# Neighbourhood-head low parts at the later place before step 32, and the addition of a head's output put off behind the maxima

## The chip, the cores and the metric

The program runs on one core of one Trainium2 chip. A core has a matrix engine (PE; its weight loads are shown apart as PEld), a vector engine (DVE), a scalar engine (ACT), a general engine (POOL) and a queue that issues transfers (SP). Each works through its own list of instructions in the order in which they were written, and waits for another engine only where a semaphore says so. The metric is the device time of one execution in microseconds (us).

## What is computed

One encoder block on 1024 tokens of width 1024, in float32. A layer norm is followed by one projection, whose columns are queries, keys and values of two attentions and two gates. The attentions run side by side: neighbourhood attention on a 16 x 64 grid (8 heads), and attention in a window of 128 tokens with 8 query heads on 2 key heads. Their outputs are projected, gated and added; a projection, a layer norm, a squared-ReLU MLP and a last layer norm follow. The change concerns the attentions alone:

```python
qa, ka, va, qb, kb, vb, ga, gb = jnp.split(proj, IN_SPLITS, axis=-1)
y_na = neighbourhood_attention(qa, ka, va, na_rpb[l]) @ w_branch_na[l]
y_swa = windowed_gqa_with_sink(qb, kb, vb, swa_sink[l]) @ w_branch_swa[l]
mixed = jax.nn.sigmoid(ga) * y_na + jax.nn.sigmoid(gb) * y_swa
# each attention, for one head:  p = softmax(q k^T / 8 + bias or mask);  o = p v
```

## The kernel before

**High and low parts.** To keep float32 accuracy, an operand of a matrix product is split in a rounded high part and the remainder, the low part: a product of the projection is three products (high by high, high by low, low by high).

**Heads and steps.** The 16 heads (8 of the window, then 8 of the neighbourhood) are worked through in 64 steps, four to a head; each handles two blocks of 128 queries. They overlap as a pipeline, written out by hand. `steps(s, n)` writes, in this order: `part_a2(s+1)` (reciprocal of the sums, L593, and scaling of the probabilities, L596), `part_a(s+2)` (scores on PE, L559 and L560; on DVE the bias is added and the maximum taken, L562, and the maxima become the exponent's offsets, L568 or L566), some matmuls of the projection, an early place where deferred work may run, `part_b(s)` (PE turns the probabilities round, L618; ACT copies them as a high part, L621; DVE subtracts for the low part `ptl`, L624) with the exponentials of step s+2 on ACT (L580, L583) between copy and subtraction, a first later place for deferred work, more matmuls, `part_c(s-1)` (probabilities times values, L654), a second later place, and the rest of the matmuls. Below, a step that "handles" k is the one whose scores are those of step k.

**What fills PE between.** `pump` writes projection matmuls (L283) of the heads to come: 12 in each step up to s = 29, 18 in each after that. `defer(n, f)` puts `f` off until n such matmuls are written; `flush` then runs it at the next place. An entry marked early may also run at the early place, ahead of `part_b`; others run only at the two later ones.

**The head's output.** Every second step two blocks of `part_c` are complete in one `ps_o` bank: the product with the high parts of the values in rows 64 to 127, with the low parts in rows 0 to 63. ACT copies one half (`evac`, L660) and DVE adds the other (`evac2`, L663), both into `oT`. There are two `ps_o` banks, used by turns; the same holds for the banks of scores (`ps_s`), of turned probabilities (`ps_t`) and of the projection (`ps_mm`).

**The neighbourhood heads' queries and keys.** When half a block of `proj_na_qk` is complete in a `ps_mm` bank, `evac` copies its high parts (ACT, L353 to L355), and `evac2`, four matmuls later, makes the low parts (DVE: L358, L360, L362).

Of the kernel before, what the change touches and what calls it, by code (L numbers as in the profile page):

```python
# [47 lines left out]
D_NA = 4  # L48
# [35 lines left out]
def encoder_block(ctx, tc, x, w_in, w_br, w_out, w_ff1, w_ff2, par, rows, rpbp,  # L84
# [4 lines left out]
    def b32(ap):  # L89
        return ap.bitcast(F32)  # L90
# [12 lines left out]
    def psum(tag):  # L103
        return pp.tile([P, 512], F32, tag=tag, name=f"ps_{tag}", bufs=PSB[tag])
# [153 lines left out]
    def h_perm(part, k, half):  # L258
        return hT[:, part, k, half * 512:(half + 1) * 512]
# [17 lines left out]
    def gemm3_steps(ps, w, act):  # L277

        hi, lo = w[:2]
        for k in range(NK):  # L280
            for i, (a, b) in enumerate(((hi, 0), (hi, 1), (lo, 0))):
                yield
                PE.matmul(ps, a[:, k, :], act(b, k), start=(k == 0 and i == 0), stop=(k == NK - 1 and i == 2))  # L283
# [6 lines left out]
    def defer(*fns, pe=False, early=False):  # L290

        later.append([fns[0], fns[1:], pe, early])

    def flush(pe=True, early=False):
        for e in list(later):
            if e[0] <= 0 and (pe or not e[2]) and (e[3] or not early):
                later.remove(e)
                e[1][0]()
                if e[1][1:]:
                    defer(*e[1][1:], early=e[3])  # L300
# [40 lines left out]
    def proj_na_qk(h, w, store):  # L341
        q = ap.tile([P, S], F32R, tag="q", name="q", bufs=3)
        kh = ap.tile([P, S], F32R, tag="kh", name="kh")
        kl = ap.tile([P, S], F32R, tag="kl", name="kl")
        store.append((q, kh, kl))
        bq, bk = prm[0:64, C_QK + h:C_QK + h + 1], prm[64:P, C_QK + h:C_QK + h + 1]
        for half in range(2):
            cs = slice(half * 512, (half + 1) * 512)
            ps = psum("mm")
            yield from gemm3_steps(ps, w, lambda part, k: h_perm(part, k, half))  # L350

            def evac(cs=cs, ps=ps):
                ACT.activation(q[0:64, cs], ps[0:64, :], AF.Identity, bias=bq, scale=1.0)  # L353
                ACT.activation(kh[64:P, cs], ps[64:P, :], AF.Identity, bias=bk, scale=1.0)
                ACT.activation(kh[0:64, cs], ps[64:P, :], AF.Identity, bias=bk, scale=1.0)  # L355

            def evac2(cs=cs, ps=ps):
                DVE.scalar_tensor_tensor(out=q[64:P, cs], in0=ps[0:64, :], scalar=bq, in1=b32(q[0:64, cs]),  # L358
                                         op0=ALU.add, op1=ALU.subtract)
                DVE.scalar_tensor_tensor(out=kl[64:P, cs], in0=ps[64:P, :], scalar=bk, in1=b32(kh[64:P, cs]),  # L360
                                         op0=ALU.add, op1=ALU.subtract)
                DVE.tensor_copy(kl[0:64, cs], b32(kl[64:P, cs]))  # L362
            defer(0, evac, D_NA, evac2, early=True)


    mk = ap.tile([P, 640], F32, tag="mk", name="mk", bufs=1)
# [20 lines left out]

    n_rope = [0]
    in_steps, rope_ops = [], []

    def rope_step(p):

        if rope_ops:
            j = cp.tile([P, 1], F32, tag="junk", name="junk", bufs=2)
            POOL.tensor_copy(j, p[:, 0:1])
            rope_ops.pop(0)()
            if len(rope_ops) % 5 == 1:
                rope_ops.pop(0)()
                if rope_ops:
                    defer(8, rope_ops.pop(0))  # L400
# [147 lines left out]
    def part_a(s):  # L548

        hd, t = heads[s // 4], s % 4  # L550
        (q, kh, kl), _, _, bias_of, sink_h, _, _ = hd.get()
        st = ap.tile([P, 8], F32, tag="st", name="st", bufs=4)
        pns = []
        for i in range(2):
            j = 2 * t + i
            c0, c1 = max(j - 1, 0), min(j + 2, 8)
            n = (c1 - c0) * P
            ps = psum("s")
            PE.matmul(ps[:, :n], q[:, j * P:(j + 1) * P], kh[:, c0 * P:c1 * P], start=True, stop=False)  # L559
            PE.matmul(ps[:, :n], q[:, j * P:(j + 1) * P], kl[:, c0 * P:c1 * P], start=False, stop=True)  # L560
            p = ap.tile([P, 384], F32, tag="ss", name="ss", bufs=6)
            DVE.tensor_tensor_reduce(out=p[:, :n], in0=ps[:, :n], in1=bias_of(j), scale=1.0, scalar=NEG,  # L562
                                     op0=ALU.add, op1=ALU.max, accum_out=st[:, i:i + 1])
            pns.append((p, n, c0))
        if sink_h is None:
            DVE.tensor_scalar(out=st[:, 2:4], in0=st[:, 0:2], scalar1=-0.125, scalar2=None, op0=ALU.mult)  # L566
        else:
            DVE.tensor_scalar(out=st[:, 2:4], in0=st[:, 0:2], scalar1=snk8[:, sink_h:sink_h + 1],  # L568
                              scalar2=-0.125, op0=ALU.max, op1=ALU.mult)
        hd.pairs[t] = pns, st  # L570
# [14 lines left out]
    def part_a2(s):  # L585
        if s >= 64:
            return
        hd, t = heads[s // 4], s % 4
        pns, st = hd.pairs[t]
        sink_h = hd.get()[4]  # L590
        if sink_h is not None:
            DVE.tensor_tensor(out=st[:, 4:6], in0=st[:, 4:6], in1=st[:, 6:8], op=ALU.add)
        DVE.reciprocal(out=st[:, 6:8], in_=st[:, 4:6])  # L593
        for i in range(2):
            p, n, c0 = pns[i]
            DVE.tensor_scalar(out=p[:, :n], in0=p[:, :n], scalar1=st[:, 6 + i:7 + i], scalar2=None, op0=ALU.mult)  # L596
        rope_step(p)
# [29 lines left out]
    def part_c(s):  # L627

        hd, t = heads[s // 4], s % 4
        order, pth, ptl = hd.pairs[t]  # L630
        _, vv, vi, _, _, o_chunk, o_row = hd.get()
        if t % 2 == 0:
            hd.po = psum("o")
        po = hd.po

        runs = []
        for u, (c, i) in enumerate(order):
            if runs and runs[-1][0] == c:
                runs[-1][2] += 1
            else:  # L640
                runs.append([c, u, 1, i])
        runs.sort(key=lambda r: -r[2])
        runs.append(runs.pop(1))
        cols_ = (t % 2) * 256
        nmm = 0
        for c, u, w, i in runs:
            cc = slice(cols_ + i * P, cols_ + (i + w) * P)
            vs = vv[:, c, vi, :, :].rearrange("p a f -> p (a f)")
            main = (po[:, cc], vs, pth[:, u:u + w, :].rearrange("p u f -> p (u f)"))
            corr = (po[0:64, cc], vs[:, 0:64], ptl[:, u:u + w, :].rearrange("p u f -> p (u f)"))  # L650
            nmm += 1
            lastrun = nmm == len(runs)
            for m in ((corr, main) if lastrun else (main, corr)):
                PE.matmul(*m, start=(nmm == 1 and m is main), stop=(lastrun and m is main))  # L654
        if t % 2 == 1:

            oo = oT[o_row:o_row + 64, o_chunk, (t // 2) * 512:(t // 2 + 1) * 512]

            def evac():
                ACT.copy(oo, po[64:P, :])  # L660

            def evac2():
                DVE.tensor_tensor(out=oo, in0=po[0:64, :], in1=oo, op=ALU.add)  # L663
            if s == 63:
                last_evac.extend((evac, evac2))
            else:
                evac()
                defer(0, evac2)

    def fills():  # L670
        def na_v_of(hp):
# [28 lines left out]
    with tc.manual_schedule(engines=MANUAL):  # L700
# [22 lines left out]
        def pump(n):  # L723
            for _ in range(n):
                if next(fill, "end") == "end":
                    for e in later:
                        e[0] = 0
                    flush()
                    return
                for e in later:  # L730
                    e[0] -= 1
# [52 lines left out]
        def steps(s, n, before_b=None, before_c=None):  # L784

            part = [int(n * SPLIT[0]), int(n * SPLIT[1])]
            part.append(n - sum(part))
            if 0 <= s + 1 < 64:
                part_a2(s + 1)
            if s + 2 < 64:  # L790
                part_a(s + 2)
            pump(part[0])
            if before_b:
                before_b()
            flush(False, True)
            if 0 <= s < 64:
                part_b(s, lambda: part_e(s + 2))
            elif s < 0:
                part_e(s + 2)
            flush(False)  # L800
            pump(part[1])
            if before_c:
                before_c()
            if s >= 1:
                part_c(s - 1)
            flush()
            pump(part[2])
# [1253 lines left out]
```

## Time and profile before

| what | value |
|---|---|
| median of 3 runs | 1334.39 us (1333.94 to 1335.63) |
| the profiled execution | 1334.06 us, of which the span of the profile 1332.3 us |
| busy share of the span | PE 98%, PEld 82%, DVE 74%, ACT 53%, POOL 21% |
| granted PE clock | 0.998 over the span |

The heads take about the stretch from 91 to 460 us: the 12-matmul steps until some 250 us, the 18-matmul steps after. In a row of the timeline stand the start, the duration, the engine, the line, the operation, the tile written and those read, and in brackets how long the engine sat idle before it and which engine's work ended that. Matmuls are pipelined, so a matmul's duration overlaps the next one's, and what PE takes is read from the distance of starts.

### The profile page before, as it was taken

What the parts mean: (1) busy time and instruction counts of PE and PEld (TensorE: products, weight loads), DVE (VectorE), ACT (ScalarE), POOL (GpSimd) and SP (SyncE); (2) the same over time, 40 slices, a digit from 0 to 9 for tenths busy, and PEclk for the clock granted to TensorE, in tenths of its full rate; (3) what the DMA queues carried; (4) which work ended last, traced back from release to release, by engine and by line L of the source; (5) the groups of instructions that cost most, each with busy time, mean ns of one, the idle gap of its engine ahead of it and who ended that gap; (6) DMA issues with size and microseconds to landing.
All of it is one profiled execution on the core that took longest, in us unless ns stands there. A gap on an engine that the chain in (4) does not pass through costs nothing.

```text
span 1332.3 us, 17348 instructions
## 1 busy us (share of the span) xinstructions
PE 1309.4 (98%) x6296; PEld 1088.7 (82%) x6296; DVE 985.0 (74%) x1618; ACT 710.1 (53%) x1231; POOL 282.4 (21%) x279
## 2 busy tenths in 40 slices
PE   8999998999999999999999999999999999999997
PEld 6788787888888878888888888888888888888886
DVE  7758888877877896444678987677655768787778
ACT  6446666766665535542445755555555543333346
POOL 4441221121120000344540012222100001111207
PEclk9999999999999999999999999999999999999999
DMA  6521111102101323656143576655528644544323
GB/s 226 187 87 49 48 52 41 38 23 47 51 23 40 127 94 118 223 190 221 70 152 134 169 242 205 210 196 187 205 100 311 221 190 150 213 150 174 127 103 127
DMA packets 66422, 183.94 MB, mean 138 GB/s; under 512 B 10400, under 2 KB 12064, under 8 KB 60576
## 3 DMA queue, kind: packets, MB, share of 16 engines
q1 hardware_dynamic: 65904, 182.38, 39.7%
q8 instruction: 49, 0.80, 0.3%
q10 hardware_dynamic: 432, 0.46, 0.1%
q14 instruction: 37, 0.30, 0.1%
HBM read 126.69 MB, written 56.31 MB: 137 GB/s over the span
## 4 chain that ended last, share of the span: by engine, by line
PE 80%; DVE 12%; ACT 3%; issue 1%; POOL 1%; DMA 1%; SPq 0%; DVEq 0%; ACTq 0%; POOLq 0%
PE ps_mm L283 13%; PE ps_mm L1351 7%; PE ps_t L1351 6%; PE ps_o L1351 6%; PE ps_mm L1784 6%; PE ps_s L1784 6%; PE ps_o L1784 5%; PE ps_t L1784 5%; PE ps_s L1351 3%; PE ps_t L618 2%; DVE ss L562 2%; PE ps_o L654 2%; ACT ss L580 2%; PE ps_mm L886 1%; DVE ss L596 1%
## 5 line engine op out<-in xcount | busy, mean ns | idle before, releaser
L283 PE MATMUL ps_mm<-hT,whi 128*128 128x512 f32 x832 | 269.5, 398 | 2.6 <-POOL hT L255 2.1
L283 PEld LDWEIGHTS ps_mm<-hT,whi 128*128 128x128 f32 x832 | 153.6, 188 | 30.2 <-POOL hT L255 3.5
L283 PE MATMUL ps_mm<-hT,wlo 128*128 128x512 f32 x416 | 166.9, 401 | 1.0 <-DVE wlo L717 1.0
L580 ACT ACTIVATE ss<-ss,st 128x384 f32<-128x384 f32 (+1 forms) x128 | 74.5, 583 | 62.1 <-DVE st L568 47.3
L1650 ACT CAST t<-stg 128x2048 fp32r<-128x2048 f32 x28 | 53.5, 1912 | 81.9 <-PE ps_o L1784 46.3
L1803 POOL TENSOR_TENSOR acc<-acc,rst 128x512 f32<-128x512 f32 x16 | 31.0, 1934 | 293.2 <-DMA rst<-xr_d 280.7
L1784 PE MATMUL ps_mm<-t,t 128*128 128x512 f32 x384 | 89.6, 389 | 0.0
L1784 PE MATMUL ps_s<-t,t 128*128 128x512 f32 x384 | 89.6, 389 | 0.0
L283 PEld LDWEIGHTS ps_mm<-hT,wlo 128*128 128x128 f32 x416 | 78.3, 188 | 12.4 <-DVE wlo L717 1.5
L1784 PEld LDWEIGHTS ps_mm<-t,t 128*128 128x128 f32 x384 | 72.1, 188 | 14.9
L1784 PEld LDWEIGHTS ps_s<-t,t 128*128 128x128 f32 x384 | 72.1, 188 | 14.9
L1351 PE MATMUL ps_t<-hS,tw 128*128 128x512 f32 x348 | 83.6, 389 | 0.0
L1351 PEld LDWEIGHTS ps_t<-hS,tw 128*128 128x128 f32 x348 | 65.3, 188 | 13.5
L621 ACT CAST pth<-ps_t 128x384 fp32r<-128x384 f32 (+1 forms) x128 | 51.8, 454 | 43.9 <-PE ps_t L618 43.2
L1653 DVE TENSOR_TENSOR t<-stg,t 128x2048 fp32r<-128x2048 f32 x28 | 65.6, 2341 | 12.9 <-ACT t L1650 12.9
L624 DVE TENSOR_TENSOR ptl<-ps_t,pth 128x384 fp32r<-128x384 f32 (+1 forms) x128 | 61.2, 517 | 17.1 <-ACT pth L621 16.5
L1173 POOL TENSOR_TENSOR mx<-sg 128x512 f32<-128x512 f32 x16 | 33.4, 2089 | 187.8 <-DVE sg L1172 187.8
L1784 PE MATMUL ps_t<-t,t 128*128 128x512 f32 x288 | 67.8, 390 | 0.6 <-DVE t L1653 0.6
L1784 PE MATMUL ps_o<-t,t 128*128 128x512 f32 x288 | 67.2, 389 | 0.0
L1784 PEld LDWEIGHTS ps_t<-t,t 128*128 128x128 f32 x288 | 53.9, 188 | 12.6 <-DVE t L1653 1.5
L1784 PEld LDWEIGHTS ps_o<-t,t 128*128 128x128 f32 x288 | 54.1, 188 | 11.2
L1627 POOL TENSOR_TENSOR rst<-rst,rr 128x512 f32<-128x512 f32 x16 | 22.4, 1400 | 187.3 <-DMA rst<-xn_d 116.0
(307 smaller groups left out, 3159.1 us busy)
## 6 DMA issues: line engine op xcount, KB each, us to landing
us_d<-usl SPq DMA_DIRECT2D x112, 256.0 KB
stg<-us_d SPq DMA_DIRECT2D x28, 1024.0 KB
raw<-in_w_ff SPq DMA_DIRECT2D x36, 512.0 KB
raw<-in_w_in SPq DMA_DIRECT2D x28, 512.0 KB
sg<-sg_d SPq DMA_DIRECT2D x32, 256.0 KB
w2b<-in_w_ff SPq DMA_DIRECT2D x7, 1024.0 KB
w2a<-in_w_ff SPq DMA_DIRECT2D x5, 1024.0 KB
sg_d<-sa SPq DMA_DIRECT2D x16, 256.0 KB
```

Of the source, the lines that this page charges most:

```text
L283: PE.matmul(ps, a[:, k, :], act(b, k), start=(k == 0 and i == 0), stop=(k == NK - 1 and i == 2))
L562: DVE.tensor_tensor_reduce(out=p[:, :n], in0=ps[:, :n], in1=bias_of(j), scale=1.0, scalar=NEG, op0=ALU.add, op1=ALU.max, accum_out=st[:, i ...
L580: ACT.activation(p[:, :n], p[:, :n], AF.Exp, bias=st[:, 2 + i:3 + i], scale=0.125, accum_out=st[:, 4 + i:5 + i])
L618: PE.transpose(pt[:, (u - a) * P:(u - a + 1) * P], p[:, (c - c0) * P:(c - c0 + 1) * P], ident)
L621: ACT.copy(pth[:, a:b, :], pv)
L624: DVE.tensor_tensor(out=ptl[:, a:b, :], in0=pv, in1=b32(pth[:, a:b, :]), op=ALU.subtract)
L1173: POOL.tensor_tensor(out=mx[:, f, half * 512:(half + 1) * 512], in0=both[0], in1=both[1], op=ALU.add)
L1351: PE.matmul(ps, ww, act[:, part, k, :], start=(first and k == 0 and m == 0), stop=(k == 3 and m == 2), skip_group_check=True)
L1650: ACT.copy(slot[:, :, 0, :], src)
L1653: DVE.tensor_tensor(out=slot[:, :, 1, :], in0=src, in1=b32(slot[:, :, 0, :]), op=ALU.subtract)
L1784: PE.matmul(ps, st[:, a, part, j * P:(j + 1) * P], w[:, a, wpart, :], start=(first and a == 0 and m == 0), stop=(a == 3 and m == 2), skip_ ...
L1803: POOL.tensor_tensor(out=z, in0=z, in1=t, op=ALU.add)
```

## The change

Two entries of deferred work are written in another way. The low parts of a neighbourhood head (`evac2` of `proj_na_qk`) were marked early always; they are now early only if their high parts were copied at a step s of 32 or more, and go to a later place before that. The DVE addition of a head's output (`evac2` of `part_c`) was deferred by 0 matmuls, which means the second later place of the same step; it is now deferred by 14.

```diff
@@ proj_na_qk
-            defer(0, evac, D_NA, evac2, early=True)
+            defer(0, lambda: (evac(), defer(D_NA, evac2, early=step_now[0] >= 32)), early=True)
@@
     n_rope = [0]
     in_steps, rope_ops = [], []
+    step_now = [0]
@@ part_c
             else:
                 evac()
-                defer(0, evac2)
+                defer(14, evac2)
@@ steps
             part = [int(n * SPLIT[0]), int(n * SPLIT[1])]
             part.append(n - sum(part))
+            step_now[0] = s
             if 0 <= s + 1 < 64:
```

No instruction is added or taken away; PE's, ACT's, POOL's and SP's lists stay as they are. On DVE, a step of 12 matmuls writes 4 after the second later place, then 3 and 5 in the next: 14 are reached in the step after the next, and the addition runs at the first later place there. In a step of 18 it runs at the second later place of the next step.

Two places on DVE show it. The first is in the window heads, the step at 150 us of the profile before. `ps_o_1492` is the output bank completed in this very step, and `ps_o_1369` (before), called `ps_o_1368` with the change, is the one completed two steps earlier. Before:

```order
L568 TENSOR_SCALAR st_1510<-st_1510,snk8_106 128x2
L624 TENSOR_TENSOR ptl_1526<-ps_t_1527,pth_1525 128x384
L624 TENSOR_TENSOR ptl_1526<-ps_t_1531,pth_1525 128x384
L663 TENSOR_TENSOR oT_844<-ps_o_1492,oT_844 64x512
L592 TENSOR_TENSOR st_1510<-st_1510 128x2
L593 RECIPROCAL st_1510<-st_1510 128x2
```

The same place with the change (a line's number is one or two higher there):

```order
L569 TENSOR_SCALAR st_1509<-st_1509,snk8_106 128x2
L625 TENSOR_TENSOR ptl_1525<-ps_t_1526,pth_1524 128x384
L625 TENSOR_TENSOR ptl_1525<-ps_t_1530,pth_1524 128x384
L664 TENSOR_TENSOR oT_844<-ps_o_1368,oT_844 64x512
L593 TENSOR_TENSOR st_1509<-st_1509 128x2
L594 RECIPROCAL st_1509<-st_1509 128x2
```

An addition still stands there, but it is that of the bank completed two steps earlier. The second place is the step in which the last window head's maxima are taken, at 248 us. Before:

```order
L568 TENSOR_SCALAR st<-st,snk_106 128x2
L358 SCALAR_TENSOR_TENSOR q<-ps_mm,prm,q 64x512
L360 SCALAR_TENSOR_TENSOR kl<-ps_mm,prm,kh 64x512
L362 CAST kl<-kl 64x512
L624 TENSOR_TENSOR ptl<-ps_t,pth 128x384 x2
L592 TENSOR_TENSOR st<-st 128x2
```

With the change:

```order
L569 TENSOR_SCALAR st<-st,snk_106 128x2
L625 TENSOR_TENSOR ptl<-ps_t,pth 128x384 x2
L358 SCALAR_TENSOR_TENSOR q<-ps_mm,prm,q 64x512
L360 SCALAR_TENSOR_TENSOR kl<-ps_mm,prm,kh 64x512
L362 CAST kl<-kl 64x512
L593 TENSOR_TENSOR st<-st 128x2
```

The low parts move behind the two `ptl` subtractions. This happens at three places (at 228, 238 and 248 us of the profile before); from step 32 on their place is unchanged.

## The prediction

> **What bounds the kernel now.** I read the page's chain by engine first, then the busy time by stretches over the heads (PE, PEld, DVE, ACT, POOL, then clock and transfers), then the chain in order of time, then the rows of PE and DVE.
>
> ```profile
> PE 80%; DVE 12%; ACT 3%; issue 1%; POOL 1%; DMA 1%; SPq 0%; DVEq 0%; ACTq 0%; POOLq 0%
> 100.00:200.00 100.00, 98.56 (x579) 83.06 (x578) 87.65 (x255) 66.73 (x176) 21.24 (x30) 1.00 0.15 50
> 200.00:256.00 56.00, 51.60 (x302) 43.07 (x302) 48.41 (x138) 40.84 (x102) 9.14 (x16) 1.00 0.14 36
> 256.00:300.00 44.00, 43.97 (x252) 37.94 (x251) 33.20 (x88) 27.37 (x61) 8.45 (x14) 1.00 0.12 31
> 300.00:400.00 100.00, 99.98 (x574) 86.47 (x573) 77.96 (x204) 64.39 (x142) 19.55 (x35) 1.00 0.15 41
> ```
>
> PE carries four fifths of the chain, at full clock. The vector engine's 12% is the opening: from 100 to 256 us DVE is busy 87.65 of 100 and 48.41 of 56, while PE falls short. From 256 us on PE is busy throughout and DVE has room. The chain just before that border shows the hand-over:
>
> ```profile
> 244.98 0.19 ACT st L583
> 245.19 0.59 ACT oT L660
> 245.81 0.68 DVE oT L663
> ...
> 248.66 0.75 DVE q L358
> ...
> 250.21 0.72 DVE kl L362
> 250.96 0.57 DVE ptl L624
> 251.57 1.01 PE ps_t L618 x6
> ```
>
> A ring of DVE and ACT sets the pace up to 251.5 us: exponentials (ACT), the output's two halves (ACT, DVE), scaling and maxima (DVE), exponentials again. PE takes over behind the low parts (L358 to L362) and the `ptl` subtraction. Both edited items stand on this chain.
>
> How much PE loses there I take from the starts of the first score matmul of each head, the only one of 256 columns that opens one:
>
> ```profile
> 106.72 0.28 PE L559 MATMUL ps_s<-kh,q 128*128 128x256 f32 x1
> 125.63 0.29 PE L559 MATMUL ps_s<-kh,q 128*128 128x256 f32 x1
> 144.84 0.39 PE L559 MATMUL ps_s<-kh,q 128*128 128x256 f32 x1 [0.17 <-DVE st L562]
> 165.97 0.39 PE L559 MATMUL ps_s<-kh,q 128*128 128x256 f32 x1 [1.13 <-DVE st L562]
> 185.28 0.39 PE L559 MATMUL ps_s<-kh,q 128*128 128x256 f32 x1
> 206.82 0.38 PE L559 MATMUL ps_s<-kh,q 128*128 128x256 f32 x1 [1.55 <-DVE st L562]
> 228.52 0.28 PE L559 MATMUL ps_s<-kh,q 128*128 128x256 f32 x1
> 249.09 0.28 PE L559 MATMUL ps_s<-kh,q 128*128 128x256 f32 x1
> 275.03 0.28 PE L559 MATMUL ps_s<-kh,q 128*128 128x256 f32 x1
> 299.97 0.28 PE L559 MATMUL ps_s<-kh,q 128*128 128x256 f32 x1
> 211.59 0.66 PE L328 MATMUL ps_t<-ident,vt 128*128 128x128 f32 x4 [0.53 <-DVE ptl L624]
> ```
>
> The heads take 18.91, 19.21, 21.13, 19.31, 21.54, 21.70 and 20.57 us with 12 matmuls a step, then 25.94 and 24.94 with 18. I take 18.91 and 24.94, the shortest, as PE's own need. The sixth head also turns two sets of values round, as the last row does (0.66 us of which the next matmuls overlap some): 2 x 0.5 us. Above need are then 0.30, 2.22, 0.40, 2.63, 1.79, 1.66 and 1.00 us: **10.0 us** that better order can give back at most.
>
> On busy time the Trainium skill speaks (Perfetto Trace Analysis, Identifying the Most-Contended Engine): matmul busy time is a poor measure of headroom, weight loads are better. By matmul busy time the rows up to 256 us would leave 1.44 + 4.40 = 5.8 us, by weight loads, against 86.47 per 100, 3.4 + 5.3 = 8.8 us; the trace agrees with the page, and I go by the starts.
>
> **The change part by part.** *The wait for the copy.* One step with an addition and the next without:
>
> ```profile
> 150.77 1.01 DVE L624 TENSOR_TENSOR ptl<-ps_t,pth 128x384 fp32r<-128x384 f32 x2
> 152.92 0.68 DVE L663 TENSOR_TENSOR oT<-ps_o,oT 64x512 f32<-64x512 f32 x1 [1.14 <-ACT oT L660]
> 153.53 0.14 DVE L592 TENSOR_TENSOR st<-st 128x2 f32<-128x2 f32 x1
> 156.07 0.87 DVE L624 TENSOR_TENSOR ptl<-ps_t,pth 128x384 fp32r<-128x384 f32 x2
> 157.72 0.16 DVE L592 TENSOR_TENSOR st<-st 128x2 f32<-128x2 f32 x1 [0.77 <-ACT st L583]
> DVE oT L663 <- ACT oT L660: 7.3, 8, 1.1
> ```
>
> The addition waits 1.14 us for ACT's copy, which stands behind the exponentials, and takes 0.68: 1.82 us between `ptl` and L592. In the step without one DVE waits 0.77 us anyway, for the last exponential. In the new order the addition in this slot is that of the bank two steps back, whose copy is long done; its 0.68 us fit in the 0.77. An addition costs nothing there and the slot shrinks by 1.82 - 0.77 = **1.05 us**. This cover is the exponentials' time; were it gone, the 0.68 would be on the ring and the slot would shrink by 0.37 only. The last row, from a list of DVE's waits up to 256 us, has eight such waits, 7.3 us: six of 1.14 and two of 0.25. Behind 144.84 us, where PE first stalls, lie four of the long ones: 4 x 1.05 = 4.2 us.
>
> *The other additions.* Three behind 144.84 us stand in slots of another kind:
>
> ```profile
> DVE vv L332 <- ACT vv L331: 3.2, 2, 2.3
> 245.81 0.68 DVE L663 TENSOR_TENSOR oT<-ps_o,oT 64x512 f32<-64x512 f32 x1 [0.25 <-ACT oT L660]
> ```
>
> Twice the addition stands right behind a wait for values that ACT is still copying (L332, 3.2 us in two, the longer 2.3, so the shorter 0.9). In the new order it stands ahead of that wait and fills it: 0.68 us each leave the ring, or less if the copy of the values should come earlier. The third had waited 0.25. Together 2 x 0.68 + 0.25 = 1.6 us.
>
> *What is saved before 144.84 us.* Two long slots and the other short one lie there, 2 x 1.05 + 0.25 = 2.35 us. PE loses almost nothing in those two heads, so this only lets DVE run closer behind it. How close it can run:
>
> ```profile
> 128.55 0.42 DVE L562 CUSTOM_DVE_ANT_0 ss<-ps_s,bd 128x256 f32<-128x256 f32 x1
> 149.19 0.42 DVE L562 CUSTOM_DVE_ANT_0 ss<-ps_s,bd 128x256 f32<-128x256 f32 x1
> 234.71 0.34 PE L559 MATMUL ps_s<-kh,q 128*128 128x384 f32 x1
> 237.14 0.55 DVE L562 CUSTOM_DVE_ANT_0 ss<-ps_s,bd 128x384 f32<-128x384 f32 x1
> ```
>
> These are the maxima of three steps whose scores started at 125.63, 144.84 and 234.71: 2.92, 4.35 and 2.43 us behind. PE stalls where the lag is above four; 2.43 is about the closest. Of the 2.35 saved, something between 0 (the lag is used up by PE's own pace) and all comes back as stalls that don't happen; the heads at 125.63 and 144.84 lost 0.30 and 2.22. I take half, **1.2 us**.
>
> *The low parts.* They take from 248.66 to 250.96, 2.30 us, ahead of `ptl`, which frees the `ps_t` banks:
>
> ```profile
> 231.02 0.33 PE L618 MATMUL ps_t<-ident,ss 128*128 128x128 f32 x1 [1.03 <-DVE ptl L624]
> 251.57 0.33 PE L618 MATMUL ps_t<-ident,ss 128*128 128x128 f32 x1 [0.81 <-DVE ptl L624]
> ```
>
> PE waits for `ptl` at two of the three moved places, 1.03 and 0.81 us. Behind `ptl` the low parts no longer hold it. What is late instead is L592 and the next maxima behind them on DVE, and with them PE's next scores; but DVE does the same work between L568 and L592 in either order, so that start doesn't move. Inside the ring this gives nothing by itself (the 1.03 is DVE's lag, counted above); at the hand-over it gives what the eighth interval is above need, **1.0 us**, as PE then waits for no one. The low parts also free `ps_mm` one `ptl` pair (1.01 us, the row at 150.77) later; the next matmuls into that bank come a half block, 24 matmuls or two steps, on, so nobody waits. With that cover gone 3 x 1.0 us would be lost.
>
> *Behind 256 us.* Sixteen additions move by a step:
>
> ```profile
> 424.14 0.43 DVE L562 CUSTOM_DVE_ANT_0 ss<-ps_s,bm 128x256 f32<-128x256 f32 x1 [1.56 <-PE ps_s L560]
> ```
>
> DVE has 10.8 us idle in the 44 us from 256 us on, and waits for PE's scores, 1.56 us here, so an addition behind other work is covered: 0. The output banks are held one step or two longer; a bank is written again three steps after its last product, and that product waits for the `ptl` just ahead of the addition, so its 0.68 us is less than PE's matmuls in between: 0.
>
> *Sum.* 4.2 + 1.6 + 1.2 + 1.0 = 8.0 us of the 10.0. The profiled execution took 1334.06, so 1326.1; it lies 0.3 below the median, hence **1326.4 us**. What follows the heads moves forward as a whole: the transfer that opens the next stage is issued when PE's last turns are done,
>
> ```profile
> 454.54 5.17 DMA graw<-in_w_in
> ```
>
> and so shifts with PE. For the range: the unsure terms at their ends give 4 x 0.37 = 1.5 us at least (no cover, nothing from the rest), and 10.0 at most.
>
> **Rivals.** (1) *PE's need alone remains.* With DVE 1.05 us per head quicker, lag never builds up again, and all 10.0 us come back: 1324.4. For it: the ring loses 4.2 + 1.6 + 2.35 + 1.0 = 9.2 us in total. Against: the heads at 144.84 and 185.28 end with splits and low parts of queries that pile up on DVE in one step; that pile stays.
>
> (2) *The addition keeps its 0.68 us on the ring*, since ACT's exponentials also end earlier or the slot is already full. Then 4 x 0.37 + 0.5 + 1.0 = 3.0 us are left (0.5 for what the early heads and the values give): 1331.4. For it: DVE is at 88% over 100 to 200 us, little room. Against: the 0.77 us wait in the step without addition.
>
> (3) *DVE's own work is the bound*, and the waits reappear elsewhere, as longer waits for the exponentials: within 1 us of before, 1334. Against: PE's stalls follow the ring's slow steps one by one.
>
> (4) *Slower: additions in front of the maxima from 256 us on.* There PE has nothing to spare; if an addition pushes L562 past PE's next scores, each of 16 costs its 0.68 us, 10.9 in all, and 10.9 - 8.0 makes it 2.9 slower: 1337.3. It decides once DVE's room in an 18-matmul step falls below 0.68 us. Against: 10.8 us idle in 44, some 1.5 us a step.
>
> (5) That the change doesn't do what it says is excluded by the order, but for its "next step", which in 12-matmul steps is the one after; this is counted in (2) and the forecast alike.
>
> **How the numbers follow.** The forecast, 6 to 9.5 us faster, has 0.60; rival 1 has 0.12, rival 2 0.18, rival 3 0.06, rival 4 0.04. A change within 0.2% (2.7 us) can't be told from none. Faster: 0.60 + 0.12 + two thirds of rival 2 = 0.84; same: the rest of rival 2 and rival 3, 0.12; slower 0.04. The range, 1324.2 to 1331.2, holds the forecast, most of rival 1 and half of rival 2.
>
> **What would show it.** The wait of L663 for L660, 7.3 us up to 256, should be nearly gone, and L592 should follow `ptl` and the addition within 0.8 us. The seven heads with 12 matmuls should take at most 19.5 us, but for the splits at the end of the third and fifth and the sixth with its turned values. PE's two waits for `ptl` behind the low parts should be gone, and the stretch behind 256 us should be as long as before. I am wrong if L592 waits longer for L583 by what L663 no longer waits, or if PE shows waits for L562 in the 18-matmul steps.

## The result

| | median of five runs, us | lowest to highest |
|---|---|---|
| before | 1335.57 | 1333.94 to 1335.90 |
| the change | 1327.06 | 1326.59 to 1327.56 |
| ratio | 0.9939 | 95% interval 0.9925 to 0.9953 |

The change is 0.6% faster, 8.5 us by these medians. The forecast was 1326.4, 8.0 us below the median known then. The profiled execution took 1326.81 us, its span 1325.0 where the one before had 1332.3.

The page's chain by engine, and the busy time by stretches (PE, PEld, DVE, ACT, POOL, then clock and transfers), answer to the first rows of the prediction. First the chain:

```profile
PE 82%; DVE 12%; ACT 3%; POOL 1%; issue 1%; DMA 1%; SPq 0%; DVEq 0%; ACTq 0%; POOLq 0%
```

Then the stretches:

```profile
100.00:200.00 100.00, 100.00 (x604) 87.55 (x602) 92.10 (x265) 71.94 (x188) 22.14 (x31) 1.00 0.16 51
200.00:249.00 49.00, 47.34 (x284) 40.65 (x283) 43.55 (x128) 35.67 (x89) 8.19 (x16) 1.00 0.13 39
300.00:400.00 100.00, 99.98 (x575) 86.29 (x573) 77.95 (x206) 64.28 (x143) 18.83 (x32) 1.00 0.12 33
```

From 100 to 200 us PE is now busy throughout, and its weight loads went from 83.06 to 87.55, about what they reach behind the hand-over (86.29). DVE is busier, 92.10 for 87.65, since the same work lies in less time. The first matmul of a head's scores, which bounded the heads in the prediction, now opens them at these times (first, sixth and tenth of the ten starts):

```profile
107.31 0.28 PE L560 MATMUL ps_s<-kh,q 128*128 128x256 f32 x1
202.26 0.38 PE L560 MATMUL ps_s<-kh,q 128*128 128x256 f32 x1 [0.56 <-DVE st L563]
292.53 0.28 PE L560 MATMUL ps_s<-kh,q 128*128 128x256 f32 x1
```

All ten starts, read in the same way in every run, give the table on which the rest stands. Each column is the time from one head's first score matmul to the next one's; the first seven have steps of 12 matmuls, the eighth holds the hand-over to steps of 18.

| kernel | nine heads, us | 1 | 2 | 3 | 4 | 5 | 6 | 7 | 8 | 9 |
|---|---|---|---|---|---|---|---|---|---|---|
| before | 193.25 | 18.91 | 19.21 | 21.13 | 19.31 | 21.54 | 21.70 | 20.57 | 25.94 | 24.94 |
| the change | 185.22 | 18.89 | 18.84 | 18.83 | 18.83 | 19.56 | 21.04 | 18.82 | 25.48 | 24.93 |
| e1, additions alone | 185.61 | 18.98 | 18.82 | 18.82 | 18.82 | 19.55 | 21.13 | 19.42 | 25.14 | 24.93 |
| e2, low parts alone | 192.27 | 18.90 | 19.22 | 21.13 | 19.28 | 21.56 | 21.72 | 19.76 | 25.77 | 24.93 |
| e4, additions after 7 | 186.50 | 18.90 | 18.79 | 18.80 | 18.79 | 19.05 | 21.05 | 19.74 | 26.43 | 24.95 |
| e5, no window additions | 183.59 | 18.98 | 18.82 | 18.82 | 18.82 | 18.82 | 20.00 | 18.82 | 25.55 | 24.96 |
| e6, window additions twice | 193.22 | 18.91 | 19.12 | 21.62 | 19.41 | 22.14 | 21.49 | 19.18 | 26.40 | 24.95 |
| e7, third low parts early | 186.45 | 18.96 | 18.79 | 18.80 | 18.79 | 19.64 | 21.12 | 18.83 | 26.58 | 24.94 |
| e8, e7 and earlier additions | 185.23 | 18.96 | 18.82 | 18.82 | 18.82 | 18.82 | 20.78 | 18.82 | 26.45 | 24.94 |
| e9, earlier additions | 184.46 | 18.90 | 18.84 | 18.83 | 18.83 | 18.84 | 20.94 | 18.83 | 25.52 | 24.93 |
| e10, low parts never early | 185.37 | 19.00 | 18.83 | 18.81 | 18.82 | 19.58 | 21.04 | 18.82 | 25.50 | 24.97 |

The change and e10 are alike in the first seven heads; their sums there, 134.81 and 134.90, differ by 0.1 us. So should those of e8 and e9, 133.84 and 134.01, where the sixth head alone differs by 0.16. Differences of 0.2 us and less are therefore not read as effects. The heads gave 193.25 - 185.22 = 8.03 us. The spans differ by 7.3, because the first of these starts came 0.6 us later in this execution (107.31 against 106.72); in the other runs it lies between 106.63 and 107.70 in no order that the edits explain.

On DVE the waits in the 12-matmul steps were, before, 7.3 us for the copy and 3.2 for values, shown in the prediction, and for the last exponential:

```profile
DVE st L592 <- ACT st L583: 7.3, 9, 1.5
```

With the change the list of DVE's waits up to 249 us is:

```profile
DVE st L593 <- ACT st L584: 7.8, 10, 1.5
DVE vv L332 <- ACT vv L331: 1.7, 1, 1.7
DVE ptl L625 <- ACT pth L622: 1.2, 2, 0.7
```

The wait of the addition for ACT's copy is gone altogether, the wait for the exponential grew by 0.5 only, and 1.2 us of waiting for the high part of the probabilities (L622) are new. The slot that the prediction worked out reads now, in the timeline of DVE:

```profile
149.18 1.01 DVE L625 TENSOR_TENSOR ptl<-ps_t,pth 128x384 fp32r<-128x384 f32 x2
150.22 0.68 DVE L664 TENSOR_TENSOR oT<-ps_o,oT 64x512 f32<-64x512 f32 x1
150.93 0.16 DVE L593 TENSOR_TENSOR st<-st 128x2 f32<-128x2 f32 x1
...
155.16 0.16 DVE L593 TENSOR_TENSOR st<-st 128x2 f32<-128x2 f32 x1 [0.77 <-ACT st L584]
```

From the end of `ptl` (150.19) to L593 it is 0.74 us, where it was 153.53 - 151.78 = 1.75: 1.01 us less. The next such slot, without an addition, still waits 0.77 for the exponential.

What the list of PE's waits still has from 90 to 460 us is three short ones:

```profile
PE ps_s L560 <- DVE st L563: 0.6, 1, 0.6
PE ps_t L328 <- DVE ptl L625: 0.5, 1, 0.5
PE ps_mm L283 <- DVE kl L360: 0.4, 1, 0.4
```

The last is new: a projection matmul waits for a bank that low parts still hold. It stands on the chain at the hand-over. With the change the chain runs over DVE and ACT up to the sixth head, and goes over to PE there, behind the low parts of the values:

```profile
209.75 0.70 DVE vv L332
...
210.50 0.44 PE ps_t L619 x2
```

It then stays on PE until 239.63, when ACT copies the high parts of a half block, and passes through `ptl` and the low parts at the hand-over:

```profile
242.25 1.02 DVE ptl L625 x2
243.27 0.03 issue
243.30 0.74 DVE q L358
244.04 0.01 issue
244.06 0.77 DVE kl L360
244.83 0.04 issue
244.87 2.11 PE ps_mm L283 x8
```

Before, the chain ran over PE for two stretches of some 7 us (from 144.84 and 185.28) and went over to it for good at the hand-over, behind `ptl`, with the low parts ahead of it. Now it comes back to PE there behind the low parts, with `ptl` ahead of them: PE waits for the projection's bank, and no longer for the probabilities.

The profiled execution of e3 below ran at a granted clock of 0.655 and took 1870.57 us, so it isn't read, and e5 is the same kernel once more.

### The profile page after: what moved, and what is told of

It reads as the page before. It is cut to its first block, busy times and chain, and to the rows that moved or that the text cites. A ratio compares the mean times of both kernels' runs of the same rounds, so it can differ in the third digit from the quotient of the medians.

```text
span 1325.0 us, 17358 instructions
## 1 busy us (share of the span) xinstructions
PE 1305.8 (99%) x6296; PEld 1089.9 (82%) x6296; DVE 989.8 (75%) x1618; ACT 709.6 (54%) x1231; POOL 284.0 (21%) x279
## 4 chain that ended last, share of the span: by engine, by line
PE 82%; DVE 12%; ACT 3%; POOL 1%; issue 1%; DMA 1%; SPq 0%; DVEq 0%; ACTq 0%; POOLq 0%
PE ps_mm L283 14%; PE ps_mm L1353 7%; PE ps_o L1353 6%; PE ps_mm L1786 6%; PE ps_t L1353 6%; PE ps_s L1786 6%; PE ps_o L1786 5%; PE ps_t L1786 5%; PE ps_s L1353 3%; PE ps_o L655 2%; PE ps_t L619 2%; PE ps_mm L888 1%; DVE ss L563 1%; DVE ss L597 1%; PE ps_s L1244 1%
## 5 line engine op out<-in xcount | busy, mean ns | idle before, releaser
L622 ACT CAST pth<-ps_t 128x384 fp32r<-128x384 f32 (+1 forms) x128 | 51.8, 455 | 50.7 <-PE ps_t L619 50.2
```

What stands on the lines that cost most here:

```text
L622: ACT.copy(pth[:, a:b, :], pv)
```

## The experiments

Names and lines are those of the change. Each edit is shown against the change; head times are in the table above.

### One half at a time: e1 and e2

```diff
 e1_additions_only
-  defer(0, lambda: (evac(), defer(D_NA, evac2, early=step_now[0] >= 32)), early=True)
+  defer(0, lambda: (evac(), defer(D_NA, evac2, early=True)), early=True)
 e2_low_parts_only
-                defer(14, evac2)
+                defer(0, evac2)
```

> Only the additions are deferred by 14; the low parts are early everywhere, as before. My sum, without its hand-over term: 4.2 + 1.6 + 1.2 = 7.0 us faster than before; over the heads (first score matmul at 107 us to that at 300 us, 193.25 us before, 185.22 with the whole change) 186.2. PE should again wait for ptl behind the third low parts, about 0.8 us, and the first two low parts should cost PE less than the 1.03 us that one of them cost before, since DVE is less late. Rival (the two edits need each other: the additions only make room for the low parts): half of it, 4 us or less.

> Only the low parts before step 32 go to the later place; additions run at once, as before. My theory: 1.0 us faster at most, all of it at the hand-over at 250 us, less what PE then waits for the low parts (0.42 us with the whole change), so 0.5 to 1.0; the ring of DVE and ACT in front of it is as long as before, with its eight waits for the copy of 7.3 us. Rival (PE's waits of 1.03 and 0.81 us for ptl are losses of their own): 1.8 us faster, the seventh head 1.0 us shorter.

e1 took 1326.81 us (1326.21 to 1327.02), ratio 0.9940 (0.9927 to 0.9953); e2 1333.95 (1333.77 to 1335.06), ratio 0.9995 (0.9986 to 1.0004). By their times e1 can't be told from the change, nor e2 from the kernel before; what the low parts do is read from the heads alone. The heads gained 193.25 - 185.61 = 7.64 us by the additions alone and 0.98 by the low parts alone. For e1 7.0 had been expected, with some 0.8 us of PE waiting for `ptl` behind the third low parts; it shows no wait there, and 0.23 us behind the first (at 224.73). For e2 the size came as expected, the place did not: 0.81 of it is in the seventh head, where the rival had put 1.0, and 0.17 at the hand-over, no more than the noise. DVE's waits in e2 show that the low parts left the ring as it was:

```profile
DVE oT L664 <- ACT oT L661: 7.3, 8, 1.1
DVE st L593 <- ACT st L584: 7.3, 9, 1.5
DVE vv L332 <- ACT vv L331: 3.2, 2, 2.3
```

So nearly all of the gain is the additions'. The two halves don't add up: 7.64 + 0.98 = 8.62, and together they give 8.03. Beside the additions the low parts gain 0.60 in the seventh head (19.42 to 18.82) and lose 0.34 in the eighth (25.14 to 25.48), where PE has its new wait of 0.42 us.

### What an addition still costs: e3, e5, e6

```diff
 e3_no_window_additions, e5_no_window_additions_again
-                defer(14, evac2)
+                if hd.n >= 8:
+                    defer(14, evac2)
 e6_window_additions_twice
-                DVE.tensor_tensor(out=oo, in0=po[0:64, :], in1=oo, op=ALU.add)
+                for _ in range(2 if hd.n < 8 else 1):
+                    DVE.tensor_tensor(out=oo, in0=po[0:64, :], in1=oo, op=ALU.add)
```

e3 and e5 leave out the half of the window heads' output that DVE adds, rows 0 to 63 of the bank; e6 adds it twice. (By the kernel these rows hold the products with the high parts of the values, which stand first in `vv`, and rows 64 to 127 those with the low parts; the description ahead of the prediction has the two the other way round. It changes nothing in the times.)

> The changed kernel with the additions of the eight window heads left out (their outputs lack one of two halves). It tells what the additions still cost in their new places. My theory: nothing in the slots that have 0.77 us of waiting, up to 0.7 us each where a slot is full (the fifth head, 19.56 us against 18.83, whose slot also has a split of weights and low parts of queries, and the sixth, 21.04, with its values): 0.7 to 1.4 us faster than the changed kernel. Rival (nowhere on the path any more): the same within 0.2 us over the heads, and the fifth head stays at 19.5.

> The changed kernel with the additions of the eight window heads left out (each output lacks one of its two halves), for its profile. The two theories of the same edit before: additions cost up to 0.7 us each where a slot is full, so the fifth head falls from 19.56 to about 18.9 and the sixth from 21.04 by up to 0.7, 0.7 to 1.4 us in all over the heads (185.22 with the whole change); or they are off the path everywhere, and the heads stay within 0.2 us. The run with the additions after 7 matmuls speaks for the first at the fifth head (19.05) and for the second at the sixth (21.05).

> The changed kernel with each addition of the window heads done twice (16 more of 0.68 us; the outputs count one half double). It tells how much room the ring of DVE and ACT has behind PE now. My cover: of two additions in a slot that waits 0.77 us only one is covered, so the ring of a head grows by 0.6 + 0.68, about 1.3 us; from the ring's lengths before, less what the change took, it now has 0 to 0.5 us of room per head, so the first five heads should get 0.8 to 1.3 us longer each from the second or third on, 4 to 6 us in all. Rival (the ring has much room, PE alone bounds): less than 1 us in all, and only at the fifth head.

Without these additions the kernel took 1326.61 us in the median of e3's other three executions (1325.47 to 1326.92; ratio 0.9938, 0.9922 to 0.9954), 0.45 less than the change, and 1325.23 in e5's one execution. The size is read from e5's heads, 183.59: 1.63 us less than the change for 14 additions of 0.68 between 107 and 250 us, 9.5 us of DVE's time; 0.7 to 1.4 had been expected. It lies in two heads, the fifth (19.56 to 18.82) and the sixth (21.04 to 20.00). Doubled, the same additions cost 8.0 us in the heads (193.22), everything that the change had gained and more than the 4 to 6 expected; the third and the fifth head alone lose 2.8 and 2.6. The timeline of DVE shows the slot of the last section with two:

```profile
152.21 1.40 DVE L665 TENSOR_TENSOR oT<-ps_o,oT 64x512 f32<-64x512 f32 x2
153.65 0.16 DVE L593 TENSOR_TENSOR st<-st 128x2 f32<-128x2 f32 x1
```

and of PE's waits the longest is again that for the maxima:

```profile
PE ps_s L560 <- DVE st L563: 4.7, 4, 2.4
```

In e5 the same slot holds no addition:

```profile
150.10 0.16 DVE L593 TENSOR_TENSOR st<-st 128x2 f32<-128x2 f32 x1 [0.53 <-ACT st L584]
```

From `ptl` to the sums it is 0.53 us without an addition, 0.74 with one and 1.47 with two. So one addition is covered but for 0.2 us (in the slots at 131 and 169 us wholly), and the second costs its whole length. In the slots that hold a split of weights and no values, which are full already, the first takes 0.6 to 0.8 us by the same comparison, and the second 0.7 to 0.9. That the heads nevertheless gain only 1.6 us from 9.5 us less of additions, and lose 8.0 from 9.8 us more (14 x 0.70), says that DVE and PE run at nearly the same pace after the change: most of what DVE saves beyond it PE cannot use, and DVE has little to spare.

Where the fifth head still loses is seen in DVE's timeline of the change, at its end:

```profile
195.85 0.94 DVE L625 TENSOR_TENSOR ptl<-ps_t,pth 128x256 fp32r<-128x256 f32 x2
196.70 0.67 DVE L664 TENSOR_TENSOR oT<-ps_o,oT 64x512 f32<-64x512 f32 x1
197.30 1.21 DVE L516 TENSOR_TENSOR wlo<-raw,whi 128x1024 fp32r<-128x1024 f32 x1
198.54 1.39 DVE L472 TENSOR_TENSOR q<-qf,q 64x512 fp32r<-64x512 f32 x2
199.96 0.35 DVE L593 TENSOR_TENSOR st<-st 128x2 f32<-128x2 f32 x1
```

The addition stands in a slot that a split of weights (L516) and the low parts of queries (L472) fill already. Nothing in it waits, so its 0.67 us are paid in full, and PE waits 0.56 at 202.26. In the sixth head of e5 PE waits for nothing, and it takes 20.00 us, 1.18 more than the shortest heads: about that is what the two turns of values take PE. The other 1.04 of the change's 21.04 go when the additions go; 0.53 of them show as PE's wait for `ptl` at 207.03.

### Another place for the additions: e4

```diff
-                defer(14, evac2)
+                defer(7, evac2)
```

> The changed kernel with the additions deferred by 7 in place of 14, so that they run one step later and not two in the steps of 12 matmuls, in slots that hold neither the split of the weights nor the turned values. The copy that they need is one step old, so no wait comes back (L664 waits for L661 0.3 us or less in all). My theory: the fifth head falls from 19.56 to about 18.9, the sixth by up to 0.7 from 21.04, so 0.7 to 1.4 us faster than the changed kernel. Rival (the piles are elsewhere: POOL's work or ACT's order makes the fifth and sixth long): no difference within 0.3 us over the heads.

1328.19 us (1327.12 to 1329.62), ratio 0.9955 (0.9941 to 0.9969); heads 186.50. This is 1.3 us more in the heads than the change, where 0.7 to 1.4 less had been expected. The fifth head gains 0.5, since the addition no longer stands in the full slot, the sixth nothing, and the seventh and eighth lose 0.92 and 0.95. There PE waits for the bank of the low parts:

```profile
234.56 0.74 PE L283 MATMUL ps_mm<-hT,whi 128*128 128x512 f32 x2 [0.57 <-DVE kl L360]
245.45 0.73 PE L283 MATMUL ps_mm<-hT,whi 128*128 128x512 f32 x2 [1.36 <-DVE kl L360]
```

After 7 matmuls the addition falls in the very slots into which the low parts were moved, and stands ahead of them. In DVE's timeline:

```profile
243.19 0.67 DVE L664 TENSOR_TENSOR oT<-ps_o,oT 64x512 f32<-64x512 f32 x1
243.88 0.74 DVE L358 SCALAR_TENSOR_TENSOR q<-ps_mm,prm,q 64x512 fp32r<-64x512 f32 x1
```

In the change the low parts follow `ptl` at once there. The best place differs from head to head, and the cover which the prediction named for the low parts ("nobody waits") is short here by 1.9 us.

### Giving that cover back: e7 and e8

If low parts behind `ptl` are what PE waits for at the hand-over, the last of the three moved ones should be better at its early place. e7 lowers the bound on the step to 28, which puts only that one back; e8 also defers the additions up to step 21 by 7, so that the one in the fifth head's full slot moves.

```diff
 e7_third_low_parts_early, e8_both_mended
-  defer(0, lambda: (evac(), defer(D_NA, evac2, early=step_now[0] >= 32)), early=True)
+  defer(0, lambda: (evac(), defer(D_NA, evac2, early=step_now[0] >= 28)), early=True)
 e8_both_mended
-                defer(14, evac2)
+                defer(7 if s < 22 else 14, evac2)
```

> The changed kernel with the bound 28 in place of 32, so that the first two low parts go to the later place and the third, the last ahead of the neighbourhood heads' steps, stays early. Theory from the runs so far (the late third holds the bank of the projection: PE waits 0.42 us for L360): that wait is gone, the eighth head falls from 25.48 to 25.14 as with the additions alone, the seventh stays at 18.8, 0.3 us faster over the heads (184.9). Rival, my prediction's: the third low parts belong behind ptl, and early they cost the hand-over, so the eighth head gets longer.

> The bound 28 and, for additions of outputs up to step 22, a delay of 7 in place of 14 (one step later, in slots without the split of the weights). If both readings hold, the fifth head is 19.05, the seventh 18.8, the eighth 25.14, and the heads take 185.2 - 0.5 - 0.3 = 184.4 us, 8.8 less than before. Rival (the two mends displace each other's waits): 185 or more.

e7 took 1327.77 us (1327.31 to 1328.01), ratio 0.9947 (0.9934 to 0.9961); e8 1328.68 (1326.73 to 1329.11), ratio 0.9952 (0.9938 to 0.9965). The eighth head did not get shorter but longer, 26.58 and 26.45 for 25.48, as the rival of e7 had it; the nine heads of e8 take 185.23 for the 184.4 expected (its rival: 185 or more). In e7 the wait for the bank is gone, and a longer one stands in its place, in PE's waits from 240 to 265 us:

```profile
PE ps_t L619 <- DVE ptl L625: 1.4, 1, 1.4
```

DVE's timeline shows why it is longer:

```profile
243.80 0.71 DVE L362 CAST kl<-kl 64x512 fp32r<-64x512 f32 x1
244.54 1.02 DVE L625 TENSOR_TENSOR ptl<-ps_t,pth 128x384 fp32r<-128x384 f32 x2
```

`ptl` ends at 245.56, against 243.27 in the change: behind all three instructions of the low parts, of which the third, which runs while POOL builds the bias of the next head, takes 0.71 us (0.42 in the change). My theory of the hand-over fell here: with DVE as late as it is there, either `ptl` or the low parts hold PE up, and `ptl` first is the cheaper, 0.42 us of waiting for 1.4. That e1, with all three low parts early, has an eighth head of 25.14 doesn't contradict it: there PE had stalled in the seventh head already (19.42), and DVE reached the same place a microsecond sooner (its L358 at 241.21, in e7 at 242.25). Over both heads e1 takes 44.56 us, the change 44.30, e7 45.41.

### Earlier additions alone: e9, and the bound itself: e10

e9 takes the one half of e8 that gained. e10 raises the bound, so that the three low parts which in the change still run ahead of `ptl` behind the hand-over (at 283, 333 and 382 us) go behind it too; the others there stand behind it already.

```diff
 e9_mixed
-                defer(14, evac2)
+                defer(7 if s < 22 else 14, evac2)
 e10_low_parts_never_early
-  defer(0, lambda: (evac(), defer(D_NA, evac2, early=step_now[0] >= 32)), early=True)
+  defer(0, lambda: (evac(), defer(D_NA, evac2, early=step_now[0] >= 100)), early=True)
```

> The change with one entry altered: the additions of the steps up to s = 21 are deferred by 7 matmuls, the later ones by 14; the low parts stay as in the change, the third ones behind ptl. If the gains at the two places are independent, the first seven heads go as they did with both places altered (fifth 18.82, sixth 20.8, seventh 18.8 us), and the eighth as in the change (25.5), since nothing is altered behind it: the nine heads take 184.2 us against 185.2, and the time is 1.0 us below the change. If instead what DVE saves in the fifth and sixth head comes back at the hand-over, because the first 18-matmul steps then begin with DVE at another lag, the eighth takes 26.4 again and the nine heads 185.2: no gain.

> The change with the bound of 32 steps raised to 100: of the twelve low parts behind the hand-over three move behind the two ptl subtractions, as the three before step 32 do in the change; nothing else moves. If low parts behind ptl hold the projection's bank beyond the next matmuls that need it (PE waited 0.42 us for them at the hand-over of the change, where its matmuls come fastest), PE, which has no spare time there, waits at each of the three places, 0.4 to 1.4 us each, and the time is 1.3 to 4.2 us above the change. If that wait was the hand-over's own and 18-matmul steps give the bank time, as the prediction had it, nothing shows: within 0.5 us of the change, with no wait of PE for L360 behind 256 us.

e9 took 1326.20 us (1325.86 to 1326.43), ratio 0.9931 (0.9917 to 0.9945); e10, on the same chip in the same series, 1327.04 (1326.79 to 1328.81), ratio 0.9940 (0.9927 to 0.9953). The ranges of the two don't meet, though the intervals of their ratios overlap. e9's heads, 184.46, came within 0.3 us of the sum put down for independent places, and its eighth is the change's, 25.52. In its timeline of DVE the addition of the fifth head left the full slot (L516 follows `ptl` at once) and stands in the next one, where the change waits 0.53 us for the exponential:

```profile
195.75 0.94 DVE L625 TENSOR_TENSOR ptl<-ps_t,pth 128x256 fp32r<-128x256 f32 x2
196.60 1.22 DVE L516 TENSOR_TENSOR wlo<-raw,whi 128x1024 fp32r<-128x1024 f32 x1
...
202.92 0.67 DVE L664 TENSOR_TENSOR oT<-ps_o,oT 64x512 f32<-64x512 f32 x1
203.53 0.22 DVE L593 TENSOR_TENSOR st<-st 128x2 f32<-128x2 f32 x1
```

So e9 is 0.8 us faster than e10 and, by its median, 0.9 faster than the change, whose heads take 0.76 more. e10 itself can't be told from the change, and its list of PE's waits has the one of the hand-over and no other for the bank:

```profile
PE ps_mm L283 <- DVE kl L360: 0.4, 1, 0.4
```

In the steady steps of 18 matmuls the place of these low parts is worth nothing that shows. The "32" matters only in that it is larger than the step of the third pair.

## Why the prediction was right, and where its terms were not

- **The bound.** The heads lost 10.0 us above PE's need, and gave back 8.03, near the 8.0 forecast. The shortest head is now 18.82, not 18.91, and the two turns of values take 1.18 (e5) and not 1.0. Against that need and 24.94, 2.4 us are left: 0.74 in the fifth head, 1.04 in the sixth, 0.54 in the eighth, little elsewhere.
- **The chain's 12%.** Read too simply: "The vector engine's 12% is the opening". The page of the change has 12% for DVE still, though 8 us of the opening are gone. Of some 165 us of DVE on the chain before, about 95 lay between 100 and 256 us, most of the rest before them and behind the heads. And since DVE now runs just ahead of PE's pace, the chain stays on DVE and ACT until 210.50, while PE is busy throughout.
- **The wait for the copy (term of 4.2).** Right in its mechanism and size: the wait, 7.3 us, is gone, and the slot shrank by 1.01 us, forecast 1.05. The four long slots shrank by 1.00, 1.31, 1.01 and 0.99 in e1, 4.3 in all. But the cover was read from another slot: the wait for the exponential is 0.53 here, not 0.77 (e5), and the addition costs 0.2 where it was to cost nothing. That the slot is 0.74 long, near the 0.77 of the forecast, is therefore partly luck: the addition sets its length and not the exponential.
- **The other additions (1.6) and the early ones (1.2).** The sixth head's slot with the longer wait for values, in DVE's timeline from the end of `ptl` to the sums, first before, then with the change:

```profile
210.98 1.01 DVE L624 TENSOR_TENSOR ptl<-ps_t,pth 128x384 fp32r<-128x384 f32 x2
215.73 0.16 DVE L592 TENSOR_TENSOR st<-st 128x2 f32<-128x2 f32 x1
```

```profile
206.42 1.01 DVE L625 TENSOR_TENSOR ptl<-ps_t,pth 128x384 fp32r<-128x384 f32 x2
210.35 0.15 DVE L593 TENSOR_TENSOR st<-st 128x2 f32<-128x2 f32 x1
```

It took 215.73 - 211.99 = 3.74 us before and takes 210.35 - 207.43 = 2.92 now, 0.82 less for 0.68 forecast. The three slots of this term shrank by 0.82, 0.81 and 0.34 in e1, 2.0 in all for 1.6, and the three slots before 144.84 us by 2.9 for 2.35. But the sixth head, which holds both waits for values, is shorter by 0.66 only, where 1.36 had been forecast. The seventh gained in its place (20.57 to 18.82 in the change, to 19.42 in e1), which fits that what DVE saves is credited to the head in which PE would next have stalled. So what each term gave PE can't be measured one by one. Their sum can: 4.2 + 1.6 + 1.2 = 7.0 forecast, 7.64 in e1, of 9.1 that these slots lost on DVE. If those behind 144.84 us count in full, 6.3, the early ones gave 1.4 of their 2.9, about the half that was taken.
- **The low parts (1.0).** This is the step that failed in its reasons. Alone they gave 0.98, as forecast, but not where forecast: 0.81 in the seventh head, "Inside the ring", where the prediction expected nothing, and 0.17 at the hand-over, which was to give the 1.0. Beside the additions they are worth 0.39. The passage "The next matmuls into that bank come a half block, 24 matmuls or two steps, on, so nobody waits" was wrong at the hand-over: PE waits 0.42 us for it, and 1.9 in e4. Most of the two steps was used up before the low parts began: ACT, behind its exponentials, copies the high parts of that bank only from 239.63 on, the low parts follow at 243.30, and PE is ready for the bank at 244.45. Behind the hand-over the passage was right (e10).
- **Why the sum held all the same.** The additions gave 0.64 more than forecast, the low parts beside them 0.61 less (0.39 for 1.0): two errors of one size and opposite signs. That the sum is right to a tenth is luck; that nearly all of it is the additions' is not.
- **Behind the hand-over.** Right: the ninth head takes 24.93 us for 24.94, and PE waits for no maxima in the steps of 18.
- **What lies behind the heads moved with them.** The transfer that opens the next stage was on the chain at 454.54 and is issued now at 447.09, 7.45 us sooner: the 8.03 of the heads less the 0.6 by which they began later.
- **The rivals.** Rival 1 (PE's need alone) was nearer than its chance says: of the five heads that had lost to DVE alone (2, 3, 4, 5 and 7) all but the fifth went to 18.8. Of the piles brought against it, that at the end of the third head is as long on DVE as before (3.17 us from `ptl` to the sums) but no longer holds PE up (18.83); that of the fifth still does. Rival 2 (the 0.68 stay on the ring) holds on DVE in the slots that are full already, but PE loses by it in the fifth and sixth heads only; e9 takes the fifth's away by moving the addition. Rival 3 falls with PE's busy time, rival 4 with the ninth head.

What stays open: which order of ACT's and DVE's work would give back the 1.04 us of the sixth head; earlier additions (e8 and e9, 20.78 and 20.94) hardly do. And what the low parts are worth beside the additions, 0.39 us in the heads of one execution each, shows in no time of a whole run.

## What to carry to other kernels

When an engine waits for a copy that another engine makes only behind its own critical work, let it do the same work one round later: it then has its data, and may fit in a wait that stands there anyway. Compare the moved piece with the wait of its own new slot (here 0.68 us against 0.53, of which 0.2 was left over), not with that of a neighbour: in a slot that is already full it costs its whole length, and here twice the piece gave back the whole gain. And where two results are due at once, ask which consumer comes first before an item is moved behind another; a place that is good in the ring can cost at the border of two stages, as in e4.

## What the runs showed of the hardware

Small instructions of DVE took longer beside POOL's work, before the change and with it. The tiny L569 (two elements a partition) runs 32 times in the window heads. In the change 15 of these take 0.53 to 0.74 us, and each of the 15 begins during a POOL instruction (L421 to L423) and ends 0.01 to 0.04 us behind it; where POOL has nothing to do it takes 0.23. DVE's timeline, then POOL's, for one:

```profile
148.53 0.73 DVE L569 TENSOR_SCALAR st<-st,snk 128x2 f32<-128x2 f32 x1
```

```profile
147.94 1.29 POOL L422 TENSOR_TENSOR qs<-qs,rt 128x512 f32<-128x512 f32 x1
```

POOL's ends at 149.23, DVE's at 149.26. The low parts' cast (L362) took 0.71 us in e7 beside POOL's additions, and 0.42 in the change where it comes later. The Trainium skill (SBUF — State Buffer, Who interferes with whom) says that DVE in some modes, which the scalar forms and casts can enter, needs a pair of ports that it shares with POOL, and that whichever of the two comes second is blocked for the whole instruction of the other; the common ends agree with it. No run here took POOL's work away, so that the ports are the cause is argued and not shown.
